# Output projection by seven block products, its weight streamed and its sums made in DRAM

## The chip, the cores and the metric

The kernel runs on one core of one Trainium2 chip. The metric is device time in microseconds (us) of one execution. Before the change three runs took 776.49, 776.52 and 776.77 us, a median of 776.52 us.

A core has a matrix engine (PE, with its weight loads shown apart as PEld), a vector engine (DVE), a scalar engine (ACT), a small general engine (POOL) and a queue engine (SP) that issues most transfers. Each runs its own list of instructions in order and waits by semaphores. 16 DMA engines carry the transfers.

## The reference

One layer of an encoder, sequence 512, width 1024, float32 throughout:

```python
h = rmsnorm(x, norm_w)
x_f, z_f, x_m, z_m, o_m, g_logits = split(h @ w_in)          # 1024 -> 10240 columns
y_a = (fourier_mix(x_f) * silu(z_f)) @ w_fourier             # 1024 x 1024
y_b = ((mlstm(x_m, o_m) + skip_w * x_c) * silu(z_m)) @ w_mlstm   # 2048 x 1024
g_a, g_b = split(sigmoid(g_logits))
x = x + (g_a * y_a + g_b * y_b) @ w_out                      # 1024 x 1024
return rmsnorm(x, final_norm_w)
```

`fourier_mix` is the real part of a two-dimensional Fourier transform, `mlstm` a matrix memory with four heads, run in chunks of 128 positions forward and backward; `x_c` is a convolved and gated `x_m`. The change concerns the product with `w_out` and the final normalization. The middle of the kernel before it stays as it was.

## The kernel before

**Arithmetic.** Each float32 matrix is split in a high and a low part: ACT copies with rounding (`hi_of`, L84), DVE subtracts (`lo_of`, L87). A product is three matmuls, high by high, high by low, low by high (`mm3`, L93 to L97).

**Weight pieces.** The table `plan` lists the weight pieces in the order of their use: 64 units of 128x1024 (512 KB each), then 55 pairs of 128x512 blocks for the block stage, then one unit and odd blocks, seven units of `w_fourier`, and at the end eight units of `w_out`. `fetch` gives each a `raw` buffer, of which there are three, and its load to SP, in the order written. `prepare` splits the piece into `whi` and `wlo`, or, for every third and fourth pair of the block stage (`extra`), into `gwh` and `gwl`; there are two buffers of each. `unit` hands out split pieces and keeps two of them ready, four while the block stage lasts. The names in the profile are those of the tiles, without buffer numbers; in the lists of instructions below they have numbers.

**Block sums in DRAM.** The block stage needs, besides weight blocks, four sums of blocks (s1 to s4) for each of its four weight groups. `sum_job` makes one: SP copies 1 MB of blocks to a DRAM tile `sums[b, k]` (L156), and POOL issues a transfer that adds another 1 MB onto it (an accumulate, L160). `unit` issues one job at every third piece from the eleventh on (`JOB_AT`, `JOB_STEP`), 17 calls in all, each with the copy of one sum and the accumulate of the sum before it.

**The block stage** (some 505 to 685 us) is the last part of the input projection, the two gates and the Fourier channels among it. The output is made in 16 groups of two tiles (`group`, L723). A group is a 2x2 block product by seven block products where the direct way has eight. The block sums of the input lie in `t_hi`, `t_lo`, `b_hi`, `b_lo`; the accumulators are X in a bank `acc`, Z and Y in banks `wk`. A product is 4 x 3 matmuls of 256 columns. The last two products of a group (`seventh`, `fourth`) are done inside the next group. ACT copies the accumulators out (L727 and L737 X, L732 Z), DVE adds (L735 and L741), and then comes the group's function, a sigmoid for the first four groups (L743).

**The merge** (L897 and below, some 685 to 730 us). For each of eight tiles j of the merged width: 24 matmuls of 512 columns by a piece of `w_fourier`, a DVE product with the gate (L910), a DVE add of the other branch (L911), a split to `m_hi[j]` and `m_lo[j]`. From j = 2 on, `split_out` splits a piece of `w_out` into its own buffers, `wo`, where all eight stay.

**The output stage** takes four row tiles t of 128 positions, two halves of 512 columns, and eight k, with three matmuls of 512 columns each (L940 to L942); the last half of t = 3 is in two pieces of 256. After each piece DVE adds the residual tile `yb` (L944), ACT squares with a sum over the row (L947), DVE multiplies by the final norm's weight `fn` (a tile `sz0`, L948). POOL adds the two sums of a row and takes the power -1/2 (`rr`, L950 to L953). ACT scales the first half (L954), DVE the second (L955), and SP stores both (L957).

**Order.** A scheduler sets the order on each engine from its own model of time. Only what is passed to `pin` (the loads of `raw`, the copies of block sums) keeps the order of the code.

Of the kernel before, what the change touches and what calls it, by code (L numbers as in the profile page):

```python
# [38 lines left out]
def hybrid_block(ctx: ExitStack, tc, xT, xn, units, blocks, vecs, gates, gbias, consts, dft, fnw, out):  # L39
# [845 lines left out]
    wo = {}

    def split_out(n):
        r = raw_unit(nplan - 8 + n)
        hi, lo = (tl(f"wo{x}{n}", [P, 2, S], F32R, pool="last") for x in "hl")
        rv = r.rearrange("p (k c) -> p k c", k=2)  # L890
        hi_of(hi, rv)
        lo_of(lo, rv, hi)
        for k2 in range(2):
            wo[2 * n + k2] = (hi[:, k2, :], lo[:, k2, :])
        fetch()
# [171 lines left out]
```

## Time and profile before

| | |
|---|---|
| median of three runs | 776.52 us |
| profiled execution: time, span | 776.38 us, 774.7 us |
| granted clock | 0.999 |
| PE busy | 763.4 us (99%), 4182 matmuls |
| PE weight loads | 647.3 us (84%) |
| DVE busy | 507.0 us (65%) |
| ACT busy | 401.0 us (52%) |
| POOL busy | 61.7 us (8%) |
| moved by the DMA engines | 117.03 MB, mean 151 GB/s |

The profiled execution is one run, recorded by the hardware. Its span reaches from the first to the last recorded instruction; 1.7 us lie around it. A row of the timeline gives the start in us, the duration in us, the engine, the line of the code, the operation, output and input tiles and shapes, and in brackets how long the engine had been idle and what released it (`[0.57 <-ACT whi L85]`). Matmuls overlap: one may be listed with 0.39 us and yet start 0.23 us after the one before, so a pace is taken from starts. A row of the table of stretches gives the stretch, its length, and for PE, PE's weight loads, DVE, ACT and POOL the busy us (and number), then the granted clock, the busy share of the DMA engines and GB/s. In the transfer view the row of a queue gives packets, MB and the share of the 16 engines' time in that window, and the row of an issue the number, the size and the us from issue to landing. q1 carries what SP issues, q0 the accumulates of POOL.

### The profile page before, as it was taken

The numbers are of one execution on the slowest core, as the hardware profiler recorded it, in microseconds if no ns is written. First come the engines' busy times: TensorE is split into PE (matmuls) and PEld (weight loads), VectorE is DVE, ScalarE is ACT, GpSimd is POOL, SyncE is SP. The second block draws the span as 40 slices with busy tenths as digits, with TensorE's granted clock in tenths as the row PEclk, the third lists the DMA queues.
The fourth block names the chain that finished last, engine by engine and source line by source line (L and its number), as shares of the span: only waits on it lengthen the run. The fifth ranks groups of instructions, "written<-read, shape, count | busy, mean of one in ns | idle before, by whom it ended". The sixth has DMA issues, their size and how long they took to land.

```text
span 774.7 us, 10917 instructions
## 1 busy us (share of the span) xinstructions
PE 763.4 (99%) x4182; PEld 647.3 (84%) x4182; DVE 507.0 (65%) x778; ACT 401.0 (52%) x629; POOL 61.7 (8%) x135
## 2 busy tenths in 40 slices
PE   8999999999999999999999999999999999999996
PEld 7876676788888888888888888899999999988885
DVE  6599876677858665866585971257666786446632
ACT  7434445659446843785363441266544587434422
POOL 0000000012100300030101000000011100000021
PEclk9999999999999999999999999999999999999999
DMA  8346782065345434346504695377654456445511
GB/s 295 135 164 190 196 227 94 3 187 156 113 113 162 136 117 129 107 110 190 163 28 163 188 292 145 83 217 215 192 160 142 133 170 192 140 154 162 168 55 55
DMA packets 39446, 117.03 MB, mean 151 GB/s; under 512 B 4577, under 2 KB 5090, under 8 KB 35298
## 3 DMA queue, kind: packets, MB, share of 16 engines
q1 hardware_dynamic: 37090, 99.56, 38.4%
q0 software_dynamic: 2304, 16.78, 11.6%
q8 instruction: 33, 0.54, 0.3%
q14 instruction: 19, 0.16, 0.1%
HBM read 114.22 MB, written 35.65 MB: 193 GB/s over the span
## 4 chain that ended last, share of the span: by engine, by line
PE 96%; ACT 1%; DVE 1%; DMA 1%; SPq 0%; issue 0%; POOL 0%; POOLq 0%; ACTq 0%
PE acc L95 17%; PE acc L97 17%; PE acc L96 17%; PE wk L97 7%; PE wk L95 7%; PE wk L96 7%; PE acc L534 3%; PE acc L535 3%; PE acc L536 3%; PE acc L942 2%; PE acc L941 2%; PE acc L940 2%; PE wk L605 2%; PE wk L292 1%; PE wk L637 1%; DMA raw<-in_units_dram 1%
## 5 line engine op out<-in xcount | busy, mean ns | idle before, releaser
L85 ACT ACTIVATE whi<-raw 128x1024 fp32r<-128x1024 f32 (+1 forms) x103 | 106.3, 1034 | 153.1 <-PE acc L96 116.3
L88 DVE TENSOR_TENSOR wlo<-raw,whi 128x1024 fp32r<-128x1024 f32 (+1 forms) x103 | 122.3, 1190 | 80.6 <-ACT whi L85 80.3
L95 PE MATMUL acc<-hhi,whi 128*128 128x512 f32 x248 | 97.2, 395 | 1.7 <-ACT whi L85 1.7
L97 PE MATMUL acc<-hhi,wlo 128*128 128x512 f32 x248 | 97.2, 393 | 0.0
L96 PE MATMUL acc<-hlo,whi 128*128 128x512 f32 x248 | 97.0, 391 | 0.0
L95 PEld LDWEIGHTS acc<-hhi,whi 128*128 128x128 f32 x248 | 46.5, 188 | 15.0 <-ACT whi L85 4.6
L97 PEld LDWEIGHTS acc<-hhi,wlo 128*128 128x128 f32 x248 | 46.6, 188 | 14.7 <-DVE sa L345 2.5
L96 PEld LDWEIGHTS acc<-hlo,whi 128*128 128x128 f32 x248 | 46.6, 188 | 10.0 <-DVE hlo L199 0.7
L536 PE MATMUL acc<-whi,hlo 128*128 128x512 f32 x128 | 50.4, 394 | 0.0
L535 PE MATMUL acc<-wlo,hhi 128*128 128x512 f32 x128 | 50.3, 393 | 0.0
L96 PE MATMUL acc<-sb,whi 128*128 128x512 f32 x128 | 49.9, 391 | 0.0
L95 PE MATMUL acc<-sa,whi 128*128 128x512 f32 x128 | 49.8, 390 | 0.1
L96 PE MATMUL wk<-vlo,phi 128*128 128x512 f32 x128 | 49.8, 389 | 0.0
L95 PE MATMUL wk<-vhi,phi 128*128 128x512 f32 x128 | 49.6, 390 | 0.0
L97 PE MATMUL acc<-sa,wlo 128*128 128x512 f32 x128 | 48.6, 391 | 0.0
L97 PE MATMUL wk<-vhi,plo 128*128 128x512 f32 x128 | 48.0, 389 | 0.0
L534 PE MATMUL acc<-whi,hhi 128*128 128x512 f32 x128 | 47.7, 393 | 0.0
L324 DVE SCALAR_TENSOR_TENSOR t2k<-sa,vecs,t2k 128x511 f32<-128x511 f32 (+1 forms) x64 | 45.6, 744 | 0.4
L88 DVE TENSOR_TENSOR gwl<-raw,gwh 128x1024 fp32r<-128x1024 f32 x27 | 33.0, 1221 | 17.3 <-ACT gwh L85 17.3
L85 ACT ACTIVATE gwh<-raw 128x1024 fp32r<-128x1024 f32 x27 | 28.6, 1059 | 19.7 <-PE acc L96 8.3
L95 PEld LDWEIGHTS wk<-vhi,phi 128*128 128x128 f32 x128 | 24.0, 188 | 5.7 <-PE acc L410 0.8
L95 PEld LDWEIGHTS acc<-sa,whi 128*128 128x128 f32 x128 | 24.0, 188 | 5.4 <-ACT whi L85 0.5
(324 smaller groups left out, 1915.8 us busy)
## 6 DMA issues: line engine op xcount, KB each, us to landing
raw<-in_units_dram SPq DMA_DIRECT2D x77, 512.0 KB, 3.8
sum<-in_blocks_dram SPq DMA_DIRECT2D x16, 1024.0 KB, 7.2
raw<-sum SPq DMA_DIRECT2D x64, 256.0 KB, 3.8
raw<-in_blocks_dram SPq DMA_DIRECT2D x48, 256.0 KB, 3.8
sum<-in_blocks_dram POOLq DMA_DIRECT2D x8, 1024.0 KB, 8.4
sum<-sum POOLq DMA_DIRECT2D x8, 1024.0 KB, 8.1
xr<-in_xT_dram SPq DMA_DIRECT2D x8, 256.0 KB, 4.3
yb<-in_xn_dram SPq DMA_DIRECT2D x8, 256.0 KB, 2.6
```

The lines of the kernel that those rows point to most:

```text
L85: se.activation(dst, src, AF.Copy, scale=scale)
L88: ve.tensor_tensor(out=dst, in0=src, in1=hi.bitcast(F32), op=ALU.subtract)
L95: pin(te.matmul(acc, wh, xh, start=start, stop=False, **skip), pinned)
L96: te.matmul(acc, wh, xl, start=False, stop=False, **skip)
L97: te.matmul(acc, wl, xh, start=False, stop=stop, **skip)
L324: ve.scalar_tensor_tensor(out=cv[:, o], in0=src[:, s], scalar=cw[k], in1=cv[:, o], op0=ALU.mult, op1=ALU.add)
L534: te.matmul(ops[t], hv(x_hi, k)[:, ts], wh[:, ks], start=k == 0, stop=False)
L535: te.matmul(ops[t], hv(x_hi, k)[:, ts], wl[:, ks], start=False, stop=False)
L536: te.matmul(ops[t], hv(x_lo, k)[:, ts], wh[:, ks], start=False, stop=k == 7)
L605: te.matmul(vp[:, ds], xm[c0 + d][:, b * P : (b + 1) * P], vbf[:, d, :], start=True, stop=True)
L940: te.matmul(acc, m_hi[k][:, ts], wh, start=k == 0, stop=False)
L941: te.matmul(acc, m_hi[k][:, ts], wl, start=False, stop=False)
```

## The change

The output projection becomes one more 2x2 block product by the scheme of seven. `w_out` is laid out as a fifth group of blocks, `blocks[4]`, with blocks of 512x512 (a11, a12, a21, a22), and four more sums of blocks are made in DRAM, `sums[4, k]`, by four more copies and four more accumulates that `unit` issues three pieces apart behind the others. `plan` ends with 14 pieces of 128x1024 where it had eight, two for each of a11, s1, a12, s2, s4, s3, a22; they go through `prepare` and `unit` as all others do, and nothing of `w_out` is kept. The rule for `extra` holds to the end of the plan, and four pieces stay ready to the end.

In the merge, the tiles j = 0 to 3 are split in their first 256 positions and in a difference of the two halves; the tiles 4 to 7 whole, and with them three sums over tiles j and j - 4. In the output stage, `wide_product` makes one block product: two row tiles by four k by three matmuls of 512 columns. The order of products is X, Z, Y, X, Z, X, X; X, Z, Y are two banks each. A product's accumulator is added to or subtracted from the residual tile, and a later product goes on adding in the same bank. Only row tile 1 is still multiplied by `fn` piece by piece (L949) and scaled at the end; the others are scaled and multiplied in one instruction of DVE (L961). The last row tile to end is t = 1, its second half in two pieces of 256. Lines of the helpers are one higher than before, those of the block stage two.

```diff
-    sums = {(b, k): dram.tile([P, 4 * S], F32, tag=f"sum{b}{k}", name=f"sum{b}{k}") for b in range(4) for k in range(4)}
+    sums = {(b, k): dram.tile([P, 4 * S], F32, tag=f"sum{b}{k}", name=f"sum{b}{k}") for b in range(NB) for k in range(4)}
...
-    plan += [[blk(NG - 1, "s3")], [units[64]], [blk(NG - 1, "a22")]] + [[units[i]] for i in range(65, 80)]
+    plan += [[blk(NG - 1, "s3")], [units[64]], [blk(NG - 1, "a22")]] + [[units[i]] for i in range(65, 72)]
+    for name in ("a11", "s1", "a12", "s2", "s4", "s3", "a22"):
+        src = sums[4, int(name[1]) - 1] if name[0] == "s" else blocks[4, {"a11": 0, "a12": 1, "a22": 3}[name]]
+        plan += [[src[:, 1024 * n : 1024 * n + 1024]] for n in range(2)]
...
     def prepare():
         i = state["split"]
-        if i >= nplan - 8:
-            return
         r = raw_unit(i)
-        extra = first_pair <= i < last_pair and i % 4 >= 2
+        extra = i >= first_pair and i % 4 >= 2
...
     def sum_job(i):
-        if i < 16:
+        if i < 4 * NB:
...
-        if i >= JOB_AT and (i - JOB_AT) % JOB_STEP == 0 and state["job"] < 17:
+        if i >= JOB_AT and (i - JOB_AT) % JOB_STEP == 0 and state["job"] <= 4 * NB:
             sum_job(state["job"])
             state["job"] += 1
-        while len(items) < (4 if "gw" in pools and state["split"] < last_pair else 2) and state["split"] < nplan - 8:
+        while len(items) < (4 if "gw" in pools else 2) and state["split"] < nplan:
             prepare()
         return items.pop(0)
...
+    def m_split(key, src):
+        shape = [src.shape[0]] + list(src.shape[1:])
+        hi, lo = (tl(f"m{key[0]}{x}{key[1]}", shape, F32R, pool="last") for x in "hl")
+        hi_of(hi, src)
+        lo_of(lo, src, hi)
+        return hi, lo
+
+    mb, mt = {}, {}
     for j in range(8):
         ga = gates_a[j]
         wh, wl = unit()
...
         ve.tensor_tensor(out=ga, in0=acc, in1=ga, op=ALU.mult)
         ve.tensor_tensor(out=ga, in0=ga, in1=mg[j], op=ALU.add)
         if j < 4:
-            if j % 2 == 0:
-                m_two = [tl(t, [P, 2, S], F32R, bufs=2) for t in ("gwh", "gwl")]
-            m_hi.append(m_two[0][:, j % 2])
-            m_lo.append(m_two[1][:, j % 2])
+            mb[0, j] = m_split(("a", j), ga[:, 0:256])
+            t0s[j] = tl(f"mx{j}", [P, 256], pool="last")
+            ve.tensor_tensor(out=t0s[j], in0=ga[:, 0:256], in1=ga[:, 256:512], op=ALU.subtract)
+            mt[0, j] = m_split(("b", j), t0s[j])
         else:
-            for m, x in ((m_hi, "h"), (m_lo, "l")):
-                m.append(tl(f"m{x}{j}", [P, S], F32R, pool="last"))
-        hi_of(m_hi[j], ga)
-        lo_of(m_lo[j], ga, m_hi[j])
-        if j >= 2:
-            split_out(j - 2)
-    for n in (6, 7):
-        split_out(n)
+            k = j - 4
+            hi, lo = m_split(("c", k), ga)
+            for n in range(2):
+                mb[1 + n, k] = hi[:, 256 * n : 256 * n + 256], lo[:, 256 * n : 256 * n + 256]
+            ts = tl("ms", [P, 3, 256], pool="last", bufs=2)
+            b12, b21, b22 = gates_a[k][:, 256:512], ga[:, 0:256], ga[:, 256:512]
+            ve.scalar_tensor_tensor(out=ts[:, 0], in0=t0s[k], scalar=-1.0, in1=b22, op0=ALU.mult, op1=ALU.subtract)
+            ve.tensor_tensor(out=ts[:, 1], in0=b22, in1=b12, op=ALU.subtract)
+            ve.scalar_tensor_tensor(out=ts[:, 2], in0=ts[:, 0], scalar=-1.0, in1=b21, op0=ALU.mult, op1=ALU.subtract)
+            hi, lo = m_split(("d", k), ts)
+            for n in range(3):
+                mt[1 + n, k] = hi[:, n], lo[:, n]
+
     res = {}
...
+    for n, (t, half) in enumerate([(0, 0), (1, 0), (2, 1), (3, 1), (2, 0), (3, 0), (0, 1), (1, 1)]):
+        res[t, half] = tl(f"yb{n}", [P, S], pool="yb")
+        nc.sync.dma_start(res[t, half], xn[t * P : (t + 1) * P, half * S : (half + 1) * S])
+
+    rows = {}
+
+    def part(t, half, cs):
+        y = res[t, half][:, cs]
+        sq = t2k()[:, 0 : cs.stop - cs.start]
+        ss = tl("fss", [P, 1], bufs=4)
+        se.activation(sq, y, AF.Square, scale=1.0 / 32.0, accum_out=ss)
+        if t not in rows:
+            rows[t] = tl("rr", [P, 1], bufs=4)
+            gp.tensor_scalar(out=rows[t], in0=ss, scalar1=EPS, scalar2=None, op0=ALU.add)
+        else:
+            gp.tensor_tensor(out=rows[t], in0=rows[t], in1=ss, op=ALU.add)
+        if t == 1:
+            ve.tensor_tensor(out=y, in0=y, in1=fn[:, half * S + cs.start : half * S + cs.stop], op=ALU.mult)
+
+    def finish(t):
+        r = rows[t]
+        gp.tensor_tensor(out=r, in0=r, in1=mhalf, op=ALU.pow)
         for half in range(2):
-            res[t, half] = tl(f"yb{2 * t + half}", [P, S], pool="yb")
-            nc.sync.dma_start(res[t, half], xn[t * P : (t + 1) * P, half * S : (half + 1) * S])
...
+            y = res[t, half]
+            if t == 1 and half == 0:
+                se.activation(y, y, AF.Copy, scale=r)
+            elif t == 1:
+                ve.tensor_scalar(out=y, in0=y, scalar1=r, scalar2=None, op0=ALU.mult)
             else:
-                gp.tensor_tensor(out=r, in0=r, in1=ss, op=ALU.add)
-        gp.tensor_tensor(out=r, in0=r, in1=mhalf, op=ALU.pow)
-        se.activation(res[t, 0], res[t, 0], AF.Copy, scale=r)
-        ve.tensor_scalar(out=res[t, 1], in0=res[t, 1], scalar1=r, scalar2=None, op0=ALU.mult)
-        for half in range(2):
-            nc.sync.dma_start(out[ts, half * S : (half + 1) * S], res[t, half])
+                ve.scalar_tensor_tensor(out=y, in0=y, scalar=r, in1=fn[:, half * S : (half + 1) * S], op0=ALU.mult, op1=ALU.mult)
+            nc.sync.dma_start(out[t * P : (t + 1) * P, half * S : (half + 1) * S], y)
+
+    full = slice(0, S)
+
+    def wide_product(accs, ms, first, pieces, then):
+        ws = [unit() for _ in range(2)]
+        for t in range(2):
+            ts = slice(t * P, (t + 1) * P)
+            for cs in pieces[t]:
+                for k in range(4):
+                    wh, wl = (v[:, k % 2 * S + cs.start : k % 2 * S + cs.stop] for v in ws[k // 2])
+                    h_, l_ = (v[:, ts] for v in ms[k])
+                    acc = accs[t][:, cs]
+                    start, stop = first and k == 0, k == 3
+                    te.matmul(acc, h_, wh, start=start, stop=False, skip_group_check=True)
+                    te.matmul(acc, h_, wl, start=False, stop=False, skip_group_check=True)
+                    te.matmul(acc, l_, wh, start=False, stop=stop, skip_group_check=True)
+                then(t, cs)
+
+    def add(accs, t0, half, op, last):
+        def then(t, cs):
+            y = res[t0 + t, half][:, cs]
+            ve.tensor_tensor(out=y, in0=y, in1=accs[t][:, cs], op=op)
+            if last:
+                part(t0 + t, half, cs)
+            if last and half == 1 and cs.stop == S:
+                finish(t0 + t)
+        return then
+
+    whole = [[full], [full]]
+    X = [bank("acc") for _ in range(2)]
+    Z = [bank("wk") for _ in range(2)]
+    Y = [bank("acc") for _ in range(2)]
+    blk4 = lambda d, n: [d[n, k] for k in range(4)]
+    wide_product(X, blk4(mb, 0), True, whole, add(X, 0, 0, ALU.add, False))
+    wide_product(Z, blk4(mt, 0), True, whole, add(Z, 2, 1, ALU.subtract, False))
+    wide_product(Y, blk4(mb, 1), True, whole, add(Y, 0, 0, ALU.add, True))
+    wide_product(X, blk4(mt, 1), False, whole, add(X, 2, 0, ALU.add, False))
+    wide_product(Z, blk4(mb, 2), False, whole, add(Z, 2, 0, ALU.add, True))
+    wide_product(X, blk4(mt, 2), False, whole, add(X, 2, 1, ALU.subtract, True))
+    wide_product(X, blk4(mt, 3), False, [[full], [slice(0, 256), slice(256, S)]], add(X, 0, 1, ALU.subtract, True))
```

The layout of `w_out` on the host changes with it. Three places of the lists of instructions follow, each as it was and as it is now.

ACT at the start of the block stage. `whi` and `gwh` are splits of weight pieces, `raw` the loaded piece, `p1`, `p5` and `u2` copies of accumulators, `pr_798` and `pr_821` (after) the first outputs of groups 0 and 1, whose in-place instruction L743, now L745, is the sigmoid; `pr_799` is group 0's second output. Before:

```order
L85 ACTIVATE whi_815_4260<-raw_809_4222 128x1024
L85 ACTIVATE whi_818_4293<-raw_812_4229 128x1024
L727 ACTIVATE p1_824_4317<-acc_823_4316 128x256
L85 ACTIVATE gwh_827_4333<-raw_817_4264 128x1024
L743 ACT_TABLE_LOAD
L743 ACTIVATE pr_798_4205<-pr_798_4205 128x512
L714 ACTIVATE pr_799_4206<-pr_799_4206 128x256
L732 ACTIVATE p5_826_4319<-wk_830_4354 128x256
L85 ACTIVATE gwh_832_4369<-raw_820_4297 128x1024
```

After:

```order
L86 ACTIVATE whi_815_4271<-raw_809_4231 128x1024
L86 ACTIVATE whi_818_4304<-raw_812_4238 128x1024
L734 ACTIVATE p5_826_4330<-wk_830_4365 128x256
L716 ACTIVATE pr_799_4213<-pr_799_4213 128x256
L739 ACTIVATE u2_825_4329<-acc_823_4327 128x256
L721 ACTIVATE pr_799_4213<-acc_800_4214 128x256
L745 ACTIVATE pr_821_4325<-pr_821_4325 128x512
L86 ACTIVATE gwh_827_4344<-raw_817_4275 128x1024
L86 ACTIVATE gwh_832_4381<-raw_820_4308 128x1024
```

The split `gwh_827`, the seventh block piece, stood ahead of group 0's sigmoid; now it stands behind group 1's.

POOL around the start of the block stage. `sum30` to `sum33` are the sums of the fourth weight group, `sum40` to `sum43` those of `w_out`, `mid` and `midl` two tiles of the Fourier part, zeroed there. Before:

```order
L160 DMA sum31_89<-sum30_88 128x2048
L160 DMA sum32_90<-in_blocks_dram 128x2048
L160 DMA sum33_91<-sum31_89 128x2048
L768 MEMSET mid_878_4699 128x256
L769 MEMSET midl_879_4700 1x128
L782 MEMSET fo_917_4940 128x2
L780 TENSOR_TENSOR fe_916_4939<-sz0_880_4703 128x2
```

After:

```order
L162 DMA sum33_91<-sum31_89 128x2048
L162 DMA sum40_92<-in_blocks_dram 128x2048
L162 DMA sum41_93<-sum40_92 128x2048
L770 MEMSET mid_878_4711 128x256
L771 MEMSET midl_879_4712 1x128
L784 MEMSET fo_917_4952 128x2
L162 DMA sum42_94<-in_blocks_dram 128x2048
L162 DMA sum43_95<-sum41_93 128x2048
L782 TENSOR_TENSOR fe_916_4951<-sz0_880_4715 128x2
```

Two of the four new accumulates stand ahead of the memset of `mid`, two behind it.

DVE at the end of the program. `yb` are the residual tiles; before, `yb6` and `yb7` are row tile 3. After, `yb4` and `yb2` are row tile 2, `yb5` and `yb3` row tile 3, `yb0` and `yb6` row tile 0, `yb7` the second half of row tile 1; L984 is the add of an accumulator. Before:

```order
L944 TENSOR_TENSOR yb6_1229_6826<-acc_1253_7035,yb6_1229_6826 128x512
L948 TENSOR_TENSOR yb6_1229_6826<-yb6_1229_6826,sz0_1156_6458 128x512
L944 TENSOR_TENSOR yb7_1230_6828<-acc_1256_7066,yb7_1230_6828 128x256
L948 TENSOR_TENSOR yb7_1230_6828<-yb7_1230_6828,sz0_1156_6458 128x256
L944 TENSOR_TENSOR yb7_1230_6828<-acc_1259_7097,yb7_1230_6828 128x256
L948 TENSOR_TENSOR yb7_1230_6828<-yb7_1230_6828,sz0_1156_6458 128x256
L955 TENSOR_SCALAR yb7_1230_6828<-yb7_1230_6828,rr_1252_7034 128x512
```

After:

```order
L984 TENSOR_TENSOR yb2_1240_6864<-yb2_1240_6864,acc_1246_6876 128x512
L961 SCALAR_TENSOR_TENSOR yb4_1242_6868<-yb4_1242_6868,rr_1289_7071,sz0_1162_6482 128x512
L961 SCALAR_TENSOR_TENSOR yb2_1240_6864<-yb2_1240_6864,rr_1289_7071,sz0_1162_6482 128x512
L984 TENSOR_TENSOR yb3_1241_6866<-yb3_1241_6866,acc_1247_6877 128x512
L984 TENSOR_TENSOR yb6_1244_6872<-yb6_1244_6872,acc_1246_6876 128x512
L961 SCALAR_TENSOR_TENSOR yb5_1243_6870<-yb5_1243_6870,rr_1292_7089,sz0_1162_6482 128x512
L961 SCALAR_TENSOR_TENSOR yb3_1241_6866<-yb3_1241_6866,rr_1292_7089,sz0_1162_6482 128x512
L984 TENSOR_TENSOR yb7_1245_6874<-yb7_1245_6874,acc_1247_6877 128x256
L961 SCALAR_TENSOR_TENSOR yb0_1238_6860<-yb0_1238_6860,rr_1272_6986,sz0_1162_6482 128x512
L961 SCALAR_TENSOR_TENSOR yb6_1244_6872<-yb6_1244_6872,rr_1272_6986,sz0_1162_6482 128x512
L949 TENSOR_TENSOR yb7_1245_6874<-yb7_1245_6874,sz0_1162_6482 128x256
L984 TENSOR_TENSOR yb7_1245_6874<-yb7_1245_6874,acc_1247_6877 128x256
```

Six scalings of whole half tiles (L961) have come between the last adds.

More of the change, by code (lines that the diff above doesn't have):

```diff
@@ L21 @@
 NG = 16
+NB = 5
 JOB_AT, JOB_STEP = 11, 3
@@ L879, in hybrid_block @@
     held.clear()
-    m_hi, m_lo = [], []
+    m_lo4, m_hi4 = {}, {}
     fn = tl("sz0", [P, D])
     nc.sync.dma_start(fn, fnw)
[L885 to L895, printed above, removed]
+    t0s = {}
+    def m_split(key, src):
[5 more added lines that the diff above has]
+    mb, mt = {}, {}
     for j in range(8):
@@ L926, in hybrid_block @@
-    res = {}
-    for t in range(4):
-        for half in range(2):
-            res[t, half] = tl(f"yb{2 * t + half}", [P, S], pool="yb")
-            nc.sync.dma_start(res[t, half], xn[t * P : (t + 1) * P, half * S : (half + 1) * S])
-    for t in range(4):
-        ts = slice(t * P, (t + 1) * P)
-        pieces = [(0, 0, S), (1, 0, S)] if t < 3 else [(0, 0, S), (1, 0, S // 2), (1, S // 2, S // 2)]
-        r = tl("rr", [P, 1], bufs=4)
-        for n, (half, c0, w) in enumerate(pieces):
-            acc = bank("acc")[:, 0:w]
-            cs = slice(c0, c0 + w)
-            for k in range(8):
-                wh, wl = (v[:, cs] for v in wo[8 * half + k])
-                te.matmul(acc, m_hi[k][:, ts], wh, start=k == 0, stop=False)
-                te.matmul(acc, m_hi[k][:, ts], wl, start=False, stop=False)
-                te.matmul(acc, m_lo[k][:, ts], wh, start=False, stop=k == 7)
-            y = res[t, half][:, cs]
-            ve.tensor_tensor(out=y, in0=acc, in1=y, op=ALU.add)
-            sq = t2k()[:, 0:w]
-            ss = tl("fss", [P, 1], bufs=4)
-            se.activation(sq, y, AF.Square, scale=1.0 / 32.0, accum_out=ss)
-            ve.tensor_tensor(out=y, in0=y, in1=fn[:, half * S + c0 : half * S + c0 + w], op=ALU.mult)
-            if n == 0:
-                gp.tensor_scalar(out=r, in0=ss, scalar1=EPS, scalar2=None, op0=ALU.add)
-            else:
-                gp.tensor_tensor(out=r, in0=r, in1=ss, op=ALU.add)
-        gp.tensor_tensor(out=r, in0=r, in1=mhalf, op=ALU.pow)
-        se.activation(res[t, 0], res[t, 0], AF.Copy, scale=r)
-        ve.tensor_scalar(out=res[t, 1], in0=res[t, 1], scalar1=r, scalar2=None, op0=ALU.mult)
-        for half in range(2):
-            nc.sync.dma_start(out[ts, half * S : (half + 1) * S], res[t, half])
@@ L999, in _layouts @@
     wo = np.asarray(inputs["w_out"])[0]
-    us += moving(wo, 0) + moving(wo, 512)
+    last = wo.reshape(2, 4, 128, 2, 512).transpose(3, 0, 2, 1, 4).reshape(1, 4, 128, 2048)
+    blocks = np.concatenate([blocks, last])
     units = np.stack(us)
```

## The prediction

> **What bounds the kernel now.** I read the page's busy times and its chain first, then the table of stretches, then the timeline where a stretch changes.
>
> ```profile
> PE 763.4 (99%) x4182; PEld 647.3 (84%) x4182; DVE 507.0 (65%) x778; ACT 401.0 (52%) x629; POOL 61.7 (8%) x135
> ...
> PE 96%; ACT 1%; DVE 1%; DMA 1%; SPq 0%; issue 0%; POOL 0%; POOLq 0%; ACTq 0%
> ```
>
> ```profile
> 500.00:550.00 50.00, 50.00 (x407) 49.03 (x407) 31.72 (x39) 31.46 (x49) 0.49 (x3) 1.00 0.66 199
> ...
> 750.00:760.00 10.00, 10.00 (x46) 8.26 (x45) 3.01 (x5) 1.70 (x5) 1.91 (x3) 1.00 0.14 52
> ...
> 768.00:774.70 6.70, 0.00 (x0) 0.00 (x0) 1.31 (x3) 1.23 (x3) 0.93 (x2) 0.85 0.21 78
> ```
>
> PE carries 96% of the chain and is never idle in the block stage or the output stage; the clock column is 1.00. So every matmul removed comes off the end, every new wait of PE goes on it, and so does whatever lengthens the last 6.7 us, where PE has stopped.
>
> **Matmuls removed.** Four rows of the output stage give the pace:
>
> ```profile
> 757.27 0.39 PE L940 MATMUL acc<-woh,gwh 128*128 128x512 f32 x1
> ...
> 759.31 0.39 PE L940 MATMUL acc<-woh,mh 128*128 128x512 f32 x1
> ...
> 762.03 0.28 PE L940 MATMUL acc<-woh,gwh 128*128 128x256 f32 x1
> ...
> 767.66 0.28 PE L942 MATMUL acc<-woh,ml 128*128 128x256 f32 x1
> ```
>
> The first two are nine matmuls apart: 2.04 / 9 = 0.227 us. The last two are 47 apart: 5.63 / 47 = 0.120 us. Before: 4 x 2 x 8 x 3 = 192 matmuls of 512 columns, 24 of them as two halves: 168 x 0.227 + 48 x 0.120 = 43.9 us. After: 7 x 2 x 4 x 3 = 168, 12 as two halves: 156 x 0.227 + 24 x 0.120 = 38.3 us. Gain 5.6 us, all on the path.
>
> **A wait removed.**
>
> ```profile
> 685.08 1.06 ACT L85 ACTIVATE whi<-raw 128x1024 fp32r<-128x1024 f32 x1 [0.40 <-PE acc L96]
> ...
> 685.22 0.40 PE L96 MATMUL acc<-fl,whi 128*128 128x512 f32 x1
> ...
> 686.19 0.50 PE L95 MATMUL acc<-fh,whi 128*128 128x512 f32 x1 [0.57 <-ACT whi L85]
> ```
>
> The split of w_fourier's second piece waited for one of two `whi` buffers, and PE lost 686.19 - 685.22 - 0.23 = 0.74 us. The new rule for `extra` gives that piece a `gwh` buffer, free before the stage begins. Gain 0.7 us.
>
> **Sums for the fifth group.** Four more copies and four more accumulates of 1 MB. What these cost is seen between 445 and 470 us, in the transfer view:
>
> ```profile
> q1 hardware_dynamic: 1099, 4.88, 48.7%
> q0 software_dynamic: 287, 2.10, 45.3%
> ...
> raw<-in_units_dram SPq DMA_DIRECT2D x5, 512.0 KB, 5.9
> sum<-in_blocks_dram POOLq DMA_DIRECT2D x1, 1024.0 KB, 8.7
> sum<-in_blocks_dram SPq DMA_DIRECT2D x1, 1024.0 KB, 10.0
> ```
>
> Two accumulates took 45.3% of 25 us: 5.7 us of all 16 engines each. By the other row a copy of 1.05 MB takes 48.7% x 25 / 4.88 x 1.05 = 2.6 us. The first two new pairs fall before 500 us, where PE needs one piece in 5.4 us, and cost nothing. The third accumulate stands on POOL behind the memset of `mid`, and the block stage then wants its pieces:
>
> ```profile
> 505.72 0.31 POOL L768 MEMSET mid<- 128x256 f32 x1 [43.81 <-PE acc L97]
> ...
> 560.76 0.39 POOL L780 TENSOR_TENSOR fe<-sz 128x2 f32<-128x2 f32 x1 [54.55 <-ACT sz L719]
> ```
>
> ```profile
> q1 hardware_dynamic: 2800, 5.10, 72.7%
> ```
>
> That is the share from 506 to 530 us before: 6.6 us free, into which come two accumulates and a copy, 14.0 us. POOL's next work is at 560 us, so POOL itself delays nobody.
>
> [...]
>
> ```profile
> q0 software_dynamic: 126, 1.02, 87.6%
> q1 hardware_dynamic: 61, 0.25, 10.6%
> issues: line engine op xcount, KB each, median us to landing
> raw<-in_units_dram SPq DMA_DIRECT2D x2, 512.0 KB, 7.9
> ```
>
> Loads got 10.6% where they will want 72.7%: 6.2 x (1 - 10.6 / 72.7) = 5.3 us late per accumulate. [...]
>
> **What this does to PE.** The scheduler has put the split of the seventh block piece (group 2's first, `gwh` 4344 in the order) behind group 1's sigmoid on ACT. Before, it ran long ahead of its reader:
>
> ```profile
> 515.56 1.06 ACT L85 ACTIVATE gwh<-raw 128x1024 fp32r<-128x1024 f32 x1
> ...
> 516.87 1.22 DVE L88 TENSOR_TENSOR gwl<-raw,gwh 128x1024 fp32r<-128x1024 f32 x1
> ...
> 518.60 0.69 DVE L752 TENSOR_TENSOR yb<-yb,pr 128x512 f32<-128x512 f32 x1 [0.51 <-ACT pr L743]
> ...
> 522.29 0.28 PE L95 MATMUL acc<-bh,gwh 128*128 128x256 f32 x1
> ...
> 524.73 0.41 DVE L741 TENSOR_TENSOR pr<-wk,u 128x256 f32<-128x256 f32 x1
> ...
> 525.18 0.63 ACT L743 ACTIVATE pr<-pr 128x512 f32<-128x512 f32 x1 [0.73 <-DVE pr L741]
> ...
> 525.72 0.36 ACT L727 ACTIVATE p<-acc 128x256 f32<-128x256 f32 x1
> ```
>
> Now the sigmoid waits for the DVE add, the add for the last product that PE has before it needs this piece. So PE stands: 0.2 to the add (see the end: last slot 767.66 + 0.12, add 767.98), 0.45 to the sigmoid (524.73 to 525.18), 0.54 to ACT's next start (to 525.72), 1.06 for the split: 2.25 us. The low part is behind a DVE product that waits for the same sigmoid (done at 1.28, plus 0.69), starts with the split's end and lasts 1.22; PE has four matmuls of 0.12 us without it, so 0.8 more. Two pieces before it (gwh 4234 behind L739, 4271 by its load, which the accumulate holds until it has landed, at 506 + 8.7) lack about 0.2 and 0.4. For the last accumulate, whose turn comes at some 522 us, I allow 0.4. Together 4.05 us. The low end is the split alone, 2.2; the high end adds both accumulates' 5.3 us less the 2.8 us that a piece lasts PE: some 8.
>
> **Streaming w_out and keeping block sums.** Fourteen pieces of 512 KB are loaded and split where eight were. A product lasts 24 x 0.227 = 5.4 us and takes two of them.
>
> ```profile
> 713.27 0.69 DVE L910 TENSOR_TENSOR y<-acc,y 128x512 f32<-128x512 f32 x1 [1.15 <-PE acc L97]
> ...
> 714.61 1.22 DVE L88 TENSOR_TENSOR wlo<-raw,whi 128x1024 fp32r<-128x1024 f32 x1
> ```
>
> The stretch from 710 to 720 us, and the loads from 690 us on:
>
> ```profile
> 710.00:720.00 10.00, 10.00 (x46) 8.29 (x45) 8.61 (x11) 3.91 (x6) 0.00 (x0) 1.00 0.78 239
> ```
>
> ```profile
> raw<-in_units_dram SPq DMA_DIRECT2D x10, 512.0 KB, 4.2
> ```
>
> Two low parts (2 x 1.22), two adds (2 x 0.69) and sometimes one product by 0.69 keep DVE 3.8 to 4.5 us of 5.4; ACT has 2 x 1.06 and squares. 1.05 MB in 5.4 us is 194 GB/s, under the 239 that moved here. In the merge DVE is worse off from j = 4 on: 2 x 0.69 + 1.22 + 3 x 0.41 + 0.69 + about 0.95 for 768 columns (between 512 and 1024) = 5.5 us per 5.4. What hides this is that the first two products read nothing of j = 4 to 7: 10.9 us of cover. Followed through the queues, the third product's first low part is ready 3 us early, the last one's 3 us. On SP a piece now stands behind the last residual load, which waits for j = 7's L911; with 4.2 us to land it comes about when its buffer is freed. I take 0, between 0 and 4.2 (one landing uncovered).
>
> **The end.**
>
> ```profile
> 756.79 0.69 DVE L944 TENSOR_TENSOR yb<-acc,yb 128x512 f32<-128x512 f32 x1 [3.21 <-PE acc L942]
> ...
> 757.58 0.63 ACT L947 ACTIVATE t2k<-yb 128x512 f32<-128x512 f32 x1 [4.72 <-DVE yb L944]
> ...
> 759.75 0.49 DVE L955 TENSOR_SCALAR yb<-yb,rr 128x512 f32<-128x512 f32 x1 [0.73 <-POOL rr L953]
> ...
> 767.98 0.42 DVE L944 TENSOR_TENSOR yb<-acc,yb 128x256 f32<-128x256 f32 x1 [1.40 <-PE acc L942]
> ...
> 770.19 0.72 ACT L954 ACTIVATE yb<-yb,rr 128x512 f32<-128x512 f32 x1 [1.19 <-POOL rr L953]
> ```
>
> From an add to the scaling of its row tile is 2.96 us (2.21 with 256 columns), through ACT and POOL. After, three row tiles finish inside the last 8 us, and DVE's order puts each tile's two scalings (L961, 0.7 us, as the 0.69 of a 512-column product) ahead of the next tile's add. With E for PE's end: the add for tile 2 waits for two low parts that follow the fifth product's add (E - 5.6 - 5.4 + 0.7 + 2 x 1.22), so E - 7.9; scalings from E - 4.9 to E - 3.5; tile 3's add; its scalings from E - 0.5 to E + 0.9; a 256-column add; two scalings of tile 0; L949: the last add starts at E + 3.1, where before it was E + 0.04. Loss 3.1 us, between 1.6 (only tile 0's two scalings and L949 in the way) and 3.4.
>
> **The sum** goes against the profiled execution, 776.38 us (span 774.7); the median of runs is 0.14 higher. - 5.6 - 0.7 + 4.05 + 0 + 3.1 = + 0.85: 777.2, by the median 777.4 us. 0.2% (1.55 us) is what can be told from no change.
>
> **Rivals.** (1) Faster: PE's wait in the block stage is covered and only 0.6 us of it stays. For it: ACT is busy 52%. Against: the split's place in ACT's order. 776.5 - 6.3 + 0.6 + 3.1 = 773.9. It decides as soon as this wait and the end together cost under 4.75 us. Chance 0.17. (2) Slower: accumulates hold pieces beyond the sigmoid. For it: 10.6% left to loads; against: at 2.8 us per piece, the next pieces are late by less than PE already stands. Another 3 us: 780.4. Chance 0.21. (3) Slower: w_out's pieces starve PE, two to three of 14 by 1 us: 779.9. For it DVE's 5.5 us; against, the cover. Chance 0.11. (4) The forecast, 775.9 to 778.4: 0.51, of which 0.04 lies above the bound. So faster 0.17, same 0.47, slower 0.36. The range, 774.5 to 780.6, leaves out the lower part of (1) and what is beyond (2).
>
> **What would show it.** PE's rows from 756 on have no gap; an idle of 2 to 3 us at some 522 us before a matmul that reads `gwh`, put down to ACT; loads near 508 and 522 us landing in 7 us; no idle at 685; the last add of DVE 3 us after PE. It is wrong if block-stage idle is over 6 or under 1.5 us, or if output products show gaps.

## The result, and the profile after

The changed kernel takes 781.27 us (median of 6, 779.69 to 782.49), the kernel before 776.67 us beside it: a ratio of 1.0058 (95% interval 1.0045 to 1.0071), slower by 0.6%. 777.4 had been forecast, 774.5 to 780.6. The profiled execution is the shortest of the six, 779.69 us with a span of 777.9 and a mean clock of 0.996; the clock of the other five is 0.994 or 0.995.

From the page after, busy times and the chain:

```profile
PE 761.2 (98%) x4146; PEld 644.8 (83%) x4146; DVE 525.5 (68%) x811; ACT 409.7 (53%) x640; POOL 65.1 (8%) x139
...
PE 93%; ACT 2%; DMA 2%; DVE 1%; issue 0%; POOL 0%; SPq 0%; POOLq 0%; ACTq 0%
```

PE fell from 96% to 93% of the chain, and DMA and ACT rose from 1% to 2% each. The table of stretches, for the start of the block stage and the end:

```profile
500.00:550.00 50.00, 45.03 (x340) 42.88 (x339) 25.29 (x31) 26.79 (x41) 2.13 (x5) 0.97 0.86 243
...
760.00:770.00 10.00, 8.48 (x44) 7.15 (x43) 6.95 (x11) 2.76 (x9) 3.96 (x7) 1.00 0.19 71
```

PE was busy for all of 500 to 550 us before; now 5.0 us are missing, and the clock column is 0.97 where it was 1.00. DMA is 0.86 busy where it was 0.66. Where PE waited, from PE's waits (in total, times, longest):

```profile
PE acc L96 <- ACT gwh L86: 2.1, 1, 2.1
...
PE wk L96 <- ACT whi L86: 1.8, 1, 1.8
PE acc L976 <- DVE yb L984: 1.5, 1, 1.5
...
PE wk L98 <- DVE wlo L89: 0.5, 1, 0.5
...
PE acc L98 <- DVE gwl L89: 0.4, 1, 0.4
```

The stages, by two instructions that both kernels have at the same place in PE's order, the last copy of an accumulator ahead of the block stage (ACT, L688, now L690) and the first product with a gate (DVE L910). Before, then after:

```profile
506.43 0.58 ACT L688 ACTIVATE yb<-acc 128x512 f32<-128x512 f32 x1
...
683.79 0.69 DVE L910 TENSOR_TENSOR y<-acc,y 128x512 f32<-128x512 f32 x1 [3.75 <-PE acc L97]
```

```profile
506.86 0.58 ACT L690 ACTIVATE yb<-acc 128x512 f32<-128x512 f32 x1
...
691.90 0.69 DVE L910 TENSOR_TENSOR y<-acc,y 128x512 f32<-128x512 f32 x1 [2.30 <-PE acc L98]
...
771.09 0.28 PE L978 MATMUL acc<-gwh,mdl 128*128 128x256 f32 x1
```

| | before | after | difference |
|---|---|---|---|
| up to the block stage | 506.43 | 506.86 | +0.43 |
| block stage to the first L910 | 177.36 | 185.04 | +7.68 |
| from there to PE's end (767.94, 771.37) | 84.15 | 79.47 | -4.68 |
| behind PE (to 774.7, 777.9) | 6.76 | 6.53 | -0.23 |

The change takes 4.7 us from the output stage, and the block stage, in which only transfers and the order of ACT and DVE have changed, gives back 7.7. It has two waits there. Rows of the timeline after:

```profile
518.33 1.06 ACT L86 ACTIVATE whi<-raw 128x1024 fp32r<-128x1024 f32 x1 [2.21 <-DMA raw<-sum]
...
519.44 0.38 PE L96 MATMUL wk<-bh,whi 128*128 128x256 f32 x1 [1.81 <-ACT whi L86]
520.70 0.38 PE L98 MATMUL wk<-bh,wlo 128*128 128x256 f32 x1 [0.52 <-DVE wlo L89]
...
528.27 0.39 PE L96 MATMUL acc<-bh,gwh 128*128 128x256 f32 x1 [2.12 <-ACT gwh L86]
529.53 0.58 PE L98 MATMUL acc<-bh,gwl 128*128 128x256 f32 x1 [0.43 <-DVE gwl L89]
```

The first is a load that is late, which the chain from 500 to 540 us shows as one piece from issue to landing:

```profile
508.62 9.63 DMA raw<-sum
```

That load ran beside the third new accumulate, which POOL issued at 506.73 us; the median of loads of this tile and size on the page is 3.8 us. The second is the place of the split behind group 1's sigmoid. And behind the second the granted clock was 0.50 for 3.41 us, as stretches of PE alone show (length, PE busy and matmuls, clock, DMA share, GB/s):

```profile
518.52:521.93 3.41, 1.97 (x14) 1.00 0.98 398
...
525.35:528.76 3.41, 1.29 (x11) 1.00 1.09 232
528.76:532.17 3.41, 2.98 (x15) 0.50 0.98 198
532.17:535.59 3.42, 3.42 (x31) 1.00 0.93 288
```

Half the clock for 3.41 us is 1.7 us at most, an estimate (0.5 x 3.41) that goes with PE's 15 matmuls in that stretch, with a wait of 0.43 us in it, and 31 in the next. With the 4.88 us of the four waits this makes 6.6; the remaining 1.1 of 7.68 are in waits too short for the list and in PE's start after each: from 519.44 to 520.70 us two matmuls at 0.12 and the wait of 0.52 account for 0.76 of 1.26 us.

### The profile page after: what moved, and what is told of

It is laid out like the page before. It is cut to its first block, busy times and chain, and to the rows that moved or that the text cites. A ratio compares the mean times of both kernels' runs of the same rounds, so it can differ in the third digit from the quotient of the medians.

```text
span 777.9 us, 10932 instructions
## 1 busy us (share of the span) xinstructions
PE 761.2 (98%) x4146; PEld 644.8 (83%) x4146; DVE 525.5 (68%) x811; ACT 409.7 (53%) x640; POOL 65.1 (8%) x139
## 4 chain that ended last, share of the span: by engine, by line
PE 93%; ACT 2%; DMA 2%; DVE 1%; issue 0%; POOL 0%; SPq 0%; POOLq 0%; ACTq 0%
PE acc L96 17%; PE acc L98 17%; PE acc L97 17%; PE wk L98 7%; PE wk L96 7%; PE wk L97 7%; PE acc L537 3%; PE acc L536 3%; PE acc L538 3%; PE wk L607 2%; PE wk L294 1%; DMA raw<-sum 1%; PE acc L978 1%; PE acc L976 1%; PE acc L977 1%; ACT whi L86 1%
## 5 line engine op out<-in xcount | busy, mean ns | idle before, releaser
L86 ACT ACTIVATE whi<-raw 128x1024 fp32r<-128x1024 f32 (+1 forms) x105 | 108.9, 1039 | 147.5 <-PE acc L97 104.0
L89 DVE TENSOR_TENSOR wlo<-raw,whi 128x1024 fp32r<-128x1024 f32 (+1 forms) x105 | 125.6, 1198 | 84.7 <-ACT whi L86 84.5
L89 DVE TENSOR_TENSOR gwl<-raw,gwh 128x1024 fp32r<-128x1024 f32 (+1 forms) x39 | 47.1, 1209 | 17.0 <-ACT gwh L86 17.0
L86 ACT ACTIVATE gwh<-raw 128x1024 fp32r<-128x1024 f32 (+1 forms) x39 | 40.8, 1047 | 28.9 <-PE acc L97 9.1
```

The source lines that it names most:

```text
L86: se.activation(dst, src, AF.Copy, scale=scale)
L89: ve.tensor_tensor(out=dst, in0=src, in1=hi.bitcast(F32), op=ALU.subtract)
```

## The experiments

**Jobs alone.** The kernel before with the four copies and accumulates, and nothing else of the change.

```diff
-        if i < 16:
-            pin(nc.sync.dma_start(sums[i // 4, i % 4], blocks[i // 4, (2, 0, 0, 1)[i % 4]], ...))
+        if i < 20:
+            pin(nc.sync.dma_start(sums[i // 4, i % 4], blocks[i // 4 % 4, (2, 0, 0, 1)[i % 4]], ...))
...
-        if i >= JOB_AT and (i - JOB_AT) % JOB_STEP == 0 and state["job"] < 17:
+        if i >= JOB_AT and (i - JOB_AT) % JOB_STEP == 0 and state["job"] < 21:
```

> The kernel before with the four further copies and accumulates alone (their sums are made in DRAM and not read; output projection, merge and end as before). ACT's order at the start of the block stage is then that of the changed kernel. Theory A: the same two waits near 519 and 528 us and the half clock, 776.6 + 7.6 to 9.2 = 784.2 to 785.8. Rival C: within 1.5 us of the kernel before, 776 to 778.

Measured 785.7 us (785.52 to 786.6), ratio 1.0119 (1.0104 to 1.0134): 9.0 us for the jobs alone, more than the whole change loses. That is what theory A expected. The profiled execution has the same waits, and two stretches at half clock. The first 50 us of its block stage, where 0.93 is what two such stretches make (2 x 3.41 x 0.5 of 50 us missing):

```profile
500.00:550.00 50.00, 45.08 (x327) 43.10 (x326) 25.11 (x30) 26.03 (x39) 2.14 (x5) 0.93 0.84 242
```

So the rest of the change gains 785.7 - 781.3 = 4.4 us, and the loss is all in the jobs.

**Order alone put back.** The changed kernel, with group 1's sigmoid queued behind the split of the seventh piece.

```diff
-        if func:
+        if func and len(n_groups) == 2:
+            with tc.issue_after(splits[first_pair + 6].ins):
+                se.activation(out0, out0, func)
+        elif func:
             se.activation(out0, out0, func)
```

> The changed kernel with one instruction of ACT moved: group 1's sigmoid behind the split of the seventh block piece (and its DVE product with it); the late accumulates stay. Theory A: the wait at 519 us, which the load of a piece causes, stays with 2.3 us; the wait at 528 (2.1 and 0.4 us) goes, and the half clock that began 0.5 us after it: 781.3 - 2.6 - 0.4 - 1.7 = 776.6 (775.5 to 778). Rival D (the piece's load is what is late and the order on ACT is only how it shows): the wait stays near 528, now put down to a transfer, 780 to 781.5.

Measured 779.5 us (778.86 to 780.43), ratio 1.0038 (1.0024 to 1.0052): 1.8 us under the changed kernel by the medians, where theory A had 4.7 less and rival D no more than 1.3 less. It lies outside both ranges. Of the 2.12 and 0.43 us at 528 us, 0.26 and 0.66 are left, and the profiled execution has no half clock before its end (0.998), yet its block stage takes 185.2 us, as long as that of the changed kernel in its profiled execution. PE's time went into other waits, 1.7 to 0.3 us long, and ACT waits for loads at 535 us. The last row below is the stretch from 505 to 535 us, with the DMA engines 0.96 busy; they were 0.71 busy there before the change and 0.96 in the changed kernel:

```profile
PE wk L96 <- ACT whi L86: 1.7, 1, 1.7
PE wk L98 <- DVE wlo L89: 1.0, 2, 0.5
PE wk L96 <- ACT p L734: 0.9, 1, 0.9
PE acc L96 <- ACT p L729: 0.7, 1, 0.7
...
535.06 1.06 ACT L86 ACTIVATE whi<-raw 128x1024 fp32r<-128x1024 f32 x1 [4.16 <-DMA raw<-in_blocks_dram]
...
505.00:535.00 30.00, 26.76 (x218) 25.62 (x217) 13.70 (x17) 14.45 (x22) 2.13 (x5) 1.00 0.96 260
```

The fourth accumulate, issued at 523.15 us, ran beside those loads as the third ran beside the first late one. With the order right, loads are the limit.

**Two accumulates out.** The changed kernel without the last two accumulates (two sums lack their second block).

```diff
-        if i > 0:
+        if 0 < i < 4 * NB - 1:
```

> The changed kernel without the last two accumulates, those that stood behind the memset of mid on POOL; their sums lack the second block, so the output differs. The copies stay. Theory G: the copy alone, 2.6 us, fits into the 6.6 us free: no wait of PE above 0.5 us from 505 to 560 us and no half clock: 772.1 to 773. Rival L (the copy of 1 MB, which stands in SP's queue ahead of the pieces, is what holds them): a wait of 2 us near 519 stays, 775 to 777.

Measured 773.18 us (772.87 to 773.91), ratio 0.9960 (0.9946 to 0.9973). One wait of 0.3 us is left in the block stage, which takes 178.49 us, 1.1 more than before. The two accumulates cost 8.1 us with what they bring, and the copy of 1 MB at most the 1.1 us that is left: no wait of 2 us near 519 us, so rival L falls. The time is 0.2 us above the range of theory G. With the accumulates went the bad order too, since the scheduler put the split ahead of group 1's sigmoid again, so this run alone doesn't part the two.

**Jobs spread.** The last four jobs at pieces 84 to 108.

```diff
-        if i >= JOB_AT and (i - JOB_AT) % JOB_STEP == 0 and state["job"] <= 4 * NB:
+        if (i >= JOB_AT and (i - JOB_AT) % JOB_STEP == 0 and state["job"] < 17) or i in (84, 92, 100, 108):
```

> The changed kernel with its sum jobs for w_out spread through the block stage: the first 17 calls as before, the last four at pieces 84, 92, 100 and 108 (some 22 us apart) instead of 62 to 71. ACT's order at the start of the block stage is then that of the kernel before. Theory G (what the block stage loses is loads: two accumulates and a copy, 14.0 us of the DMA engines, come into 24 us that have 6.6 us free; where they have 22 us each, nothing is lost): no wait of PE from 505 to 685 us, no half clock, 779.7 - 7.6 = 772.1 (771.5 to 773.0). Rival H (any accumulate in the block stage, wherever it stands, makes PE wait 2 us): three accumulates stand there, 778.

Measured 773.24 us, ratio 0.9964 (0.9950 to 0.9979): faster than before, and 0.2 us above the range of theory G. The profiled execution took 771.58 us, and its block stage 177.33 us, as before the change:

```profile
500.00:550.00 50.00, 50.00 (x408) 49.03 (x407) 31.97 (x39) 31.59 (x49) 0.49 (x3) 1.00 0.68 200
550.00:600.00 50.00, 50.00 (x421) 48.31 (x420) 31.71 (x64) 22.48 (x38) 7.80 (x20) 1.00 0.83 245
```

Three accumulates lie in the block stage here and PE loses nothing, so rival H falls. But ten runs spread from 771.39 to 776.09 us, and none of the long ones was profiled. The next kernel's profile shows one way in which such a run loses time.

**Jobs spread, and the end changed.** The last half in one piece, and row tile 0's scalings behind the last add.

```diff
-    wide_product(X, blk4(mt, 3), False, [[full], [slice(0, 256), slice(256, S)]], add(X, 0, 1, ALU.subtract, True))
+    wide_product(X, blk4(mt, 3), False, whole, add(X, 0, 1, ALU.subtract, True))
...
-            if last and half == 1 and cs.stop == S:
+            if last and half == 1 and t0 + t > 0:
                 finish(t0 + t)
+            if last and half == 1 and t0 + t == 1:
+                with tc.issue_after(adds[-1].ins):
+                    finish(0)
```

> Spread sum jobs and the end of the run before together (last half in one piece, row tile 0's scalings behind the last add). In the profiled executions the end gave 0.84 us (PE 1.92 earlier after the merge, 1.08 more behind PE). Theory: the two add up, 772.1 - 0.8 = 771.3 (770.5 to 772.2). Rival E (the end is set by DVE): as with spread jobs alone, 772.1.

Measured 771.58 us (771.45 to 773.9), ratio 0.9945 (0.9931 to 0.9958), the best together with the dense one below. The profiled execution was one of the two long ones, 773.31 us, and shows where it lost 2.5 us:

```profile
570.58 1.23 DVE L89 TENSOR_TENSOR wlo<-raw,whi 128x1024 fp32r<-128x1024 f32 x1 [5.19 <-ACT whi L86]
571.72 0.16 DVE L789 COPY fe<-so 128x2 f32<-128x2 f32 x1
...
572.03 0.91 PE L796 MATMUL wk<-dch,fe 128*128 128x129 f32 x6 [2.49 <-DVE fe L789]
```

From 559 to 567 us an accumulate had 72.3% of the DMA engines' time, and a load issued at 558.63 us took 10.76 us to land, by the chain; the low part of that piece stands on DVE ahead of a 0.16 us copy for the Fourier part, and PE waited 2.5 us for the copy.

**The end alone.** The same change of the end on the changed kernel.

> The changed kernel with the last half of row tile 1 in one piece of 512 columns instead of two of 256, and the two scalings of row tile 0 behind the last add on DVE. Theory A: PE's wait of 1.5 us inside the last product (second piece behind DVE's add from the same bank) goes, what comes after PE grows by 0.4 us: 781.3 - 1.1 = 780.2, with the scatter of the changed kernel (779 to 781). Rival E (the end is set by DVE's scalings, not by PE): no change, 781.3.

Measured 781.05 us (778.3 to 781.73), ratio 1.0050 (1.0032 to 1.0068): by the times nothing can be told, since the block stage scatters by more. The profiled executions tell it: from the first L910 to PE's end 77.55 us where it was 79.47, and 7.64 us behind PE where it was 6.53, a gain of 0.8.

**Order alone made bad.** The spread kernel, with the split of the seventh piece forced behind group 1's sigmoid.

```diff
+            if len(n_groups) == 2:
+                tc.add_manual_dep(splits[first_pair + 6].ins, sig.ins.name, ...)
```

> The spread kernel (sum jobs for w_out at pieces 84 to 108) with ACT's order forced to that of the changed kernel at one place: the split of the seventh block piece behind group 1's sigmoid. Loads are in time there. Theory A, the term of the prediction (the chain product, DVE add, sigmoid, split, low part stands on PE's path by itself): a wait of 2.1 and 0.4 us near 523 to 525 us put down to ACT, and in most executions a stretch at clock 0.5 behind it: 773.2 + 2.6 to 4.7 = 775.8 to 777.9. Theory G alone (only missing loads cost): 773.2, no wait there.

Measured 781.31 us (779.35 to 782.21), ratio 1.0056 (1.0041 to 1.0071): as slow as the changed kernel, and above what either theory expected. It isn't a clean copy of that order: against the spread kernel two more splits went behind the sigmoid, and against the changed kernel one later split stands ahead of it. But the DMA engines have room. PE's wait, the stretch in which it falls, with DMA at 0.40 and the half clock behind it, and DVE's rows ahead of the sigmoid:

```profile
PE acc L96 <- ACT gwh L86: 4.2, 1, 4.2
...
523.90:527.31 3.41, 0.06 (x1) 0.06 (x1) 2.46 (x5) 1.73 (x4) 0.00 (x0) 1.00 0.40 109
527.31:530.73 3.42, 3.42 (x16) 3.37 (x17) 3.06 (x3) 1.90 (x2) 0.00 (x0) 0.50 0.41 103
...
523.42 1.22 DVE L89 TENSOR_TENSOR wlo<-raw,whi 128x1024 fp32r<-128x1024 f32 x1 [3.56 <-ACT whi L86]
...
525.17 0.42 DVE L743 TENSOR_TENSOR pr<-wk,u 128x256 f32<-128x256 f32 x1
```

PE stopped at 523.0 us, and the add that the sigmoid waits for began at 525.17, behind the low part of that later split. So about 2.0 of the 4.2 us come from the later split and, as an estimate, 2.2 from the place of the seventh, near the 2.25 of the prediction. The execution has the 2.6 us wait for the Fourier copy as well. So the order costs PE time without any shortage of loads, an estimated 2.2 us and up to 1.7 more (3.42 us at 0.50 here) where the clock halved behind it; the late loads without the bad order cost 7.9 (the order put back). Together, in the changed kernel, they cost 7.7 in the profiled execution, no more than the loads alone: putting one right shows little, 1.8 us by the medians, while the other stands.

**Jobs at every second piece.** All sums early.

```diff
-JOB_AT, JOB_STEP = 11, 3
+JOB_AT, JOB_STEP = 11, 2
```

> The changed kernel with its block sums made every second piece instead of every third (JOB_STEP 2), so that all twenty are in DRAM before the block stage; on ACT the split of the seventh block piece then stands ahead of the first sigmoid again. Theory A (two late accumulates and the place of that split make PE wait 4.9 us at 519 and 528 us, and the half clock after the waits is the rest): both waits and every stretch at clock 0.5 inside the span are gone, 781.3 - 8.8 = 772.5 us (771.6 to 773.3). Rival B (the clock falls by itself, from the load on the chip): only the waits go, with 1.0 us for refilling, 775.4, and clock 0.994 stays. Rival C (the loss lies in the streamed output stage and the end): above 779.

Measured 777.85 us (775.19 to 779.36), ratio 1.0011 (1.0000 to 1.0022). The block stage is clean, 177.34 us, but 6 us are lost before it: DVE's order around 440 us had changed, an input load on SP waited for DVE, and weight loads stood behind it. SP issued that load at 447.07 us, where the changed kernel issued it at 439.67, and from 440 to 445 us the DMA engines moved nothing: the loads came late here without a shortage of the engines.

```profile
447.04 1.06 ACT L86 ACTIVATE th<-xs 128x1024 fp32r<-128x1024 f32 x1 [4.98 <-DVE xs L667]
...
454.15 1.06 ACT L86 ACTIVATE whi<-raw 128x1024 fp32r<-128x1024 f32 x1 [3.07 <-DMA raw<-in_units_dram]
...
449.75:453.16 3.41, 1.32 (x6) 1.00 0.85 303
453.16:456.57 3.41, 1.31 (x3) 0.50 0.42 172
456.57:459.98 3.41, 3.41 (x9) 0.50 0.47 160
```

PE waited 4.2 us and ran at half clock for 6.82 us. The time fits neither A nor the two rivals: moving jobs moved the scheduler's order at a place nobody had named.

**Jobs 2.3 pieces apart, and the end changed.** Calls at pieces 11 to 57; DVE keeps its order around 440 us.

```diff
+        if i in (11, 13, 15, 17, 20, 22, 24, 27, 29, 31, 34, 36, 38, 40, 43, 45, 47, 50, 52, 54, 57):
```

> The changed kernel with all 21 calls of sum jobs 2.3 pieces apart (pieces 11 to 57), so that every accumulate is over before the block stage, and the end of the run with the last half in one piece. Theory G: no wait of PE from 505 us on and none in the w_mlstm stage, 771.3 (770.5 to 772) with less scatter than the spread kernel. Rival M (2.3 pieces apart is too dense: loads are held in the mLSTM or w_mlstm stage, as they were with jobs at every second piece): a wait of 1 us or more before 505 us, 773 to 776.

Measured 771.78 us (770.65 to 772.82), ratio 0.9939 (0.9926 to 0.9951). This is inside the range of theory G and under that of rival M. The block stage takes 177.34 us. Five runs spread over 2.2 us, and the five of the spread kernel with the same end over 2.5, so less scatter is not shown. In the profiled execution some 2 us are lost ahead of the block stage (508.57 at the copy that was at 506.43), and not by a held load, as rival M has it:

```profile
194.70 0.85 POOL L162 DMA_DIRECT2D sum<-sum  x1 [4.16 <-DMA sum<-in_blocks_dram]
...
196.51 0.49 DVE L629 TENSOR_SCALAR so<-so,rr 128x512 f32<-128x512 f32 x1 [4.60 <-POOL rr L628]
```

An accumulate stands on POOL ahead of a norm's power (`rr`) and waited 4.16 us for the copy that it adds to, DVE waited for `rr`, and PE came 2.0 us late between 197 and 202 us. The longest wait of PE there is 0.5 us.

**Waits put in.** The kernel before, with the high parts of four pieces written again by ACT.

```diff
+        for _ in range({53: 4, 56: 5, 59: 6, 62: 8}.get(i, 0)):
+            hi_of(hi[:, 0:w], hi[:, 0:w].bitcast(F32))
```

> The kernel before with four waits of PE put into the w_mlstm stage, 440 to 505 us, where the DMA engines have room: the high part of pieces 53, 56, 59 and 62 is copied onto itself by ACT 4, 5, 6 and 8 times. Waits of some 0.7, 1.8, 3 and 6 us of PE (estimated from 1.06 us a copy and 5.4 us of cover). Theory K (a wait of some 2 us or more halves the clock for one or more stretches of 3.41 us behind it, at a loss of 1.7 us each): stretches at 0.5 behind the two or three longest waits and none behind the first, time 776.7 + waits + 1.7 per stretch, some 792. Rival B (the clock falls from the load of the chip): no stretch at 0.5, some 788.

Measured 792.57 us, ratio 1.0211 (1.0197 to 1.0225). Stretches of PE around three of the waits:

```profile
444.37:447.78 3.41, 2.18 (x10) 1.00 0.91 375
447.78:451.20 3.42, 3.27 (x15) 1.00 0.62 103
464.85:468.26 3.41, 1.54 (x6) 1.00 0.96 197
468.26:471.67 3.41, 3.41 (x10) 0.50 0.75 245
485.33:488.74 3.41, 1.73 (x6) 1.00 0.00 0
488.74:492.15 3.41, 2.94 (x7) 0.50 0.51 153
```

With PE busy for 2.18 of 3.41 us the clock stayed at 1.00; with 1.54 and 1.73 the next 3.41 us ran at 0.50. The DMA engines stood still in one of them (0.00), so rival B falls: here the clock halved behind a wait, without load from transfers. The waits came out otherwise than estimated: 1.2 and 3.0 us, then 0.9, 0.8 and 0.5 in place of 3, then 0.9 and 3.0 in place of 6. The three short ones, none of them theory K's 2 us, had the half clock from 488.74 us behind them. The last two fell into two stretches, 505.81 to 509.22 and 509.22 to 512.63 us, with PE busy for 1.36 and 1.53 us, and the 3.41 us behind each of them ran at half clock, so that there are four at half clock in all. The time is theory K's 792 and not B's 788.

## Why the prediction was wrong, point by point

- **Matmuls removed, -5.6, and the wait at 685 us, -0.7: right.** From the first L910 to PE's end it is -4.68 = -5.6 - 0.84 + 1.76, with 1.76 for a wait of the end (below). The wait at 685 us is gone and was worth 0.84 with PE's start after it.
- **Streaming, 0: right.** PE's list has no wait of a product of w_out for a piece.
- **The block stage, +4.05: the step that failed; 7.68 measured.** The piece at fault and its chain were named rightly: 2.25 and 0.8 us forecast, 2.12 and 0.43 measured. What failed are the "0.2 and 0.4" for the pieces before it, which made PE wait 1.81 and 0.52 us, and what the prediction put at nothing: the half clock, up to 1.7, and some 1.1 in short waits and PE's start after each. The "0.4" for the last accumulate left no wait on the list. Putting the order right showed more: without the sigmoid in the way the accumulates cost the same 7.9 us. The prediction had the figures: 14.0 us of transfers into 6.6 us of room leave 7.4 us over. It priced a chain of instructions and treated the shortage as an allowance on it, where by three runs the shortage was the bound: the DMA engines 0.96 busy for 30 us with the order put back, 1.1 us lost without the two accumulates, none with the jobs spread. That 7.4 comes so near to 7.7 and 7.9 is no check of the sum, since the half clock is in the first and not in the second. Its high end of 8 was near the measured 7.68, but with 8 its own sum is 781.3 us, above the 780.6 at which its range ends. The 6.2 us in its 5.3 us per accumulate are one accumulate's stay before, from 450.3 to 456.5 us, the time of the two queue rows with 87.6% and 10.6%; after, the load beside the third accumulate took 9.63 us to land, where the median is 3.8.
- **The clock: not in the prediction.** Its rows had 1.00 up to PE's end, and PE's longest wait from 500 us to there was 0.6 us. One stretch at half clock was up to 1.7 of the 7.68 us. The median is 1.6 above the profiled execution, with a lower mean clock; a second stretch, as in the profiled executions of the jobs alone and the end alone, would make that difference, but no profile of the other five runs shows it.
- **The end, +3.1: mis-sized, +1.5 measured.** DVE's scalings did come ahead of the adds. But the last two pieces of 256 columns share a bank, and PE waited for the add of the first:

```profile
769.21 0.41 DVE L984 TENSOR_TENSOR yb<-yb,acc 128x256 f32<-128x256 f32 x1
...
769.68 0.39 PE L976 MATMUL acc<-whi,mdh 128*128 128x256 f32 x1 [1.52 <-DVE yb L984]
...
771.41 0.42 DVE L984 TENSOR_TENSOR yb<-yb,acc 128x256 f32<-128x256 f32 x1
```

DVE worked off its scalings while PE waited, so the last add began 0.04 us behind PE and not 3.1. "No gap" in PE's rows "from 756 on" was wrong. That this term came out 1.6 us lower than forecast was luck: it hides part of the 3.6 us by which the block stage was too low.
- **The rivals.** The number lies nearest to (2), accumulates that hold pieces beyond the sigmoid, 780.4 at 0.21. In the changed kernel itself the held piece stood ahead of that sigmoid, and PE's list has no wait of the block stage behind the split's two. Only with the order put back do the pieces beyond it keep PE waiting (near 536 us), and what was set against (2), "the next pieces are late by less than PE already stands", fails there: the fourth accumulate came while the DMA engines were still full with what the third had held (0.98 busy from 522.31 to 525.72 us).

## What to carry to other kernels

When a change adds transfers to a stretch, set their time against the free time of that stretch first: if they don't fit, expect a loss of the order of the excess (7.4 us here, by the view of before, with 7.7 and 7.9 lost), whatever chain shows it; here untying one chain moved the wait to the next. Spread such transfers until each has its own room: the same bytes cost 9.0 us as jobs alone at pieces 62 to 71, and nothing in the block stage at pieces 84 to 108 in the profiled execution, though runs of that kernel spread over 4.7 us. After each move read the order again: four jobs moved a split behind a sigmoid, jobs at every second piece moved DVE's order 60 us earlier, and an accumulate that waited 4.16 us for its copy held a norm's power behind it on POOL. And in six profiled executions waits that left PE busy for 0.06 to 1.73 of 3.41 us had 3.41 us at half clock behind them (one stretch with 1.63 had not): where a change brings waits like these, allow up to 1.7 us on top, an estimate (0.5 x 3.41).

## What the runs showed of the hardware

Ahead of PE's end the half clock came in stretches of 3.41 us that started on one grid in a run: 468.26 and 488.74 us, with the waits put in, are six of them apart (20.48 us), and the two of the jobs alone, 520.64 and 530.88 us, three (10.24 us). A stretch of the grid in which PE was busy for 1.73 of 3.41 us (the waits put in, from 485.33 us) had the next at half clock; stretches with 1.77 (the order put back, 515.48 to 518.90 us) and 1.97 (the changed kernel, 518.52 to 521.93 us) had not; where the line runs was not settled, nor whether busy time alone decides (one stretch with 1.63, in the kernel with the order made bad from 575.10 to 578.50 us, had not either). The grid did not start at the same place in every run: a stretch of it began at 517.23 us in the jobs alone and at 518.52 us in the changed kernel, and nearly the same waits near 519 us had the half clock behind them in one and not in the other. In the jobs alone, 1.7 and 0.5 us long, they left PE busy for 1.23 us of one stretch, and the next ran at 0.50; in the changed kernel, 1.81 and 0.52 us long, they fell into two with 2.52 and 1.97, and the clock stayed at 1.00. This may be one source of the scatter; the runs don't show how much of it.

Beside an accumulate, loads got little of the DMA engines in the stretches measured: from 559 to 567 us in the spread kernel with the other end the accumulate had 72.3% of the engines' time and q1, with the loads and copies, 20.4%, and from 508.3 to 514.8 us after, 82.4% and 13.1%.

```profile
q0 software_dynamic: 136, 1.02, 82.4%
q1 hardware_dynamic: 148, 0.28, 13.1%
```
